# Weight units of 128x2048 in half as many buffers, in a fp32 two-block transformer on one core

## The chip, the core and the metric

The kernel runs on one core of a Trainium2 chip. Its engines are TensorE (PE: matmuls and transposes into PSUM), VectorE (DVE), ScalarE (ACT), GpSimd (POOL) and SyncE (SP), which here issues the loads of the weights. The metric is the device time of one execution in microseconds. The trace and its views come from one profiled execution.

## The reference, cut to what matters

256 tokens of 1024 features go through two blocks, all in fp32. The matrices are the weights that the change is about.

```python
# first block
h = rmsnorm(x, norm_mix)
(q, kc, vc, ks, vs, kw, vw, nsa_g, rq, rk, rv, rg, gate_a, gate_b) = split(h @ w_in)
nsa_out = nsa_mixer(rotary(q), rotary(kc), vc, ...)   # compress(): silu(blocks(k) @ ck_w1) @ ck_w2
ret_out = silu(rg) * retention(rq, rk, rv)
mix = sigmoid(gate_a) * (nsa_out @ w_proj_a) + sigmoid(gate_b) * (ret_out @ w_proj_b)
x = x + mix @ w_out
h = rmsnorm(x, norm_mlp)
x = x + square(relu(h @ w_up)) @ w_down               # hidden width 4096
x = rmsnorm(x, norm_final)
# second block
n = rmsnorm_2(h)
z, xBC, dt, q, k, v, r, a1, g_ssd, g_gla = split(n @ w_in)
merged = sigmoid(g_ssd) * (ssd_mixer(...) @ w_up_ssd) + sigmoid(g_gla) * (gla_mixer(...) @ w_up_gla)
h = h + merged @ w_o
h = h + mem_cross_attention(rmsnorm_2(h), rmsnorm_2(mem), w_xq, w_xkv, w_xo)
h = h + (silu(g) * u) @ w_ffn_out                     # g, u = split(rmsnorm_2(h) @ w_ffn_in), width 2816
return rmsnorm_2(h, norm_final)
```

## The kernel before

**Precision.** TensorE is to multiply fp32 values, but in its fp32r format. So each operand is split in a high part (a cast to fp32r) and a low part (the value less its high part), and each product is three matmuls: high by high, high by low, low by high. `load` does this for one unit of weights: SyncE loads it into a buffer `raw`, ScalarE casts `wh`, VectorE subtracts `wl` (L95 to L97 of before, L99 to L101 of after). A unit is 128 rows by up to UNIT columns: some 128-row blocks of a weight matrix, beside each other. Activations are split alike (`split`, L113) into pairs such as `hh`/`hl`, `gd`/`k2`.

**Buffers.** Each kind of tile has a ring of buffers (BUFS); a tile waits until an older one of its ring is free. `raw` has 4, `wh` and `wl` have 8 each, of 128x1024. So a unit's load waits for the subtraction of an older unit, and its cast for the matmuls of an older unit.

**Order.** The program writes the operations in an order of its own, and a framework then schedules each engine's queue, before the run, with the rings as one of its constraints. On each engine the instructions run in the order of that queue, which the sections below show in a few places.

**The GEMMs.** `gemm_tok` makes a token-major product of two column ranges for both halves of the tokens (it holds all its weights until the second half is done); `gemm_feat` and `s_feat` make feature-major products of 256 columns; `s_tok` is a token-major product of 512 columns that yields after each pair of 128-row blocks. The `stream` is a list of such products (`stream1`: rq, rk, rv, rg and the gates) from which other code draws pieces (`pump`, `need`), as work for TensorE while NSA or retention runs on other engines.

**NSA's prologue.** After the first norm, kv and q are projected (`gemm_tok`, 512 columns) and the gates and windows (280 columns). Keys are rotated (L356 to L359), doubled (L434), transposed and split. `compress` builds blocks of keys (L374, L381, L113) and multiplies them by `ck_w1` and later `cv_w1`, each in four loads of four 128-row blocks by 256 columns. rq and rk come from the stream at the same time; their rows are rotated on VectorE by the same lines L356 to L359 (128x512).

**w_down and w_ffn_out** (`Down`): the hidden rows come in parts of two 128-row blocks by 1024 columns. All but the last parts are added into four accumulators (two halves t of the tokens, two halves f of the columns) as they come. The last parts are held back (`late`), and then `finish` runs them half by half: all of (0, 0) and (0, 1), then the residual add (L845) and the norm of the first 128 tokens (squares L218, L220, L211 on GpSimd, products L230), while TensorE does (1, 0) and (1, 1). After w_down two norms follow each other, and then the transposes for the next projection.

Of the kernel before, what the change touches and what calls it, by code (L numbers as in the profile page):

```python
# [12 lines left out]
F32 = mybir.dt.float32  # L13
# [7 lines left out]
P = 128  # L21
EPS = 1e-6
NEG = -1e30
NUNITS = 314
UNIT = 1024
WARM = 14


# [6 lines left out]
G_MIX, G_MLP, G_FIN, G_MIX2, G_XATT, G_MEM, G_FFN, G_FIN2, G_SSD, G_GLA, G_NUM = range(11)  # L35

BUFS = dict(
    raw=4, wh=8, wl=8, hh=5, hl=5, xr=2, g2=9, k2=14, gd=10, sc=24,
)


# [10 lines left out]
class Builder:  # L52
# [36 lines left out]
    def load(self, w, c0, ncol, k, nk):  # L89
        nc = self.nc  # L90
        i = len(self.keys)
        self.keys.append((w, c0, ncol, k, nk))
        raw, wh, wl = self.T("raw", [P, UNIT]), self.T("wh", [P, UNIT], F32R), self.T("wl", [P, UNIT], F32R)
        m = nk * ncol
        nc.sync.dma_start(raw[:, :m], self.d["wbig"][i, :, :m])  # L95
        nc.scalar.copy(wh[:, :m], raw[:, :m])  # L96
        nc.vector.tensor_sub(wl[:, :m], raw[:, :m], wh[:, :m].bitcast(F32))  # L97
        cs = [slice(j * ncol, (j + 1) * ncol) for j in range(nk)]
        return [(wh[:, c], wl[:, c]) for c in cs]  # L99

    def units(self, w, c0, ncol, K, k0=0):  # L101
        n = UNIT // ncol
        return [x for k in range(k0, k0 + K, n) for x in self.load(w, c0, ncol, k, min(n, k0 + K - k))]

    def mm(self, out, lhsT, rhs, start, stop):
        self.nc.tensor.matmul(out, lhsT, rhs, start=start, stop=stop)  # L106
# [13 lines left out]
            self.mm(o, hi, wl, False, False)  # L120
            self.mm(o, lo, wh, False, k == K - 1)

    def gemm_tok(self, w, c0s, ncol, src, K=8, rest=None, mid=None, ahead=3, others=()):

        us, n = [], UNIT // ncol
        for c0 in c0s:
            us.append([])
            for k in range(0, K, n):  # L130

                with ExitStack() as order:
                    if rest and (c0 != c0s[0] or k >= ahead * n):
                        for x in self.first:
                            order.enter_context(self.tc.issue_after(x.ins))
                    us[-1] += self.load(w, c0, ncol, k, min(n, K - k))
                if c0 == c0s[0] and k // n in others:
                    others[k // n]()
        acc = [[self.PS("acc") for _ in range(2)] for _ in c0s]
        for t in range(2):  # L140
            if rest and t:
                rest()
            for g in range(len(c0s)):
                if mid and t and g == len(c0s) - 1:
                    mid(acc)
                self.tok_mm(acc[g][t][:, :ncol], src, us[g], t)
        return acc

    def s_tok(self, key, w, c0, ncol, src, done, K=8):

        acc = [self.PS("acc") for _ in range(2)]
        n = UNIT // ncol
        for k0 in range(0, K, n):
            ws = self.load(w, c0, ncol, k0, min(n, K - k0))
            for t in range(2):
                o = acc[t][:, :ncol]
                for j, (wh, wl) in enumerate(ws):
                    k = k0 + j
                    hi, lo = src.parts(k, slice(t * P, (t + 1) * P))
                    self.mm(o, hi, wh, k == 0, False)  # L160
                    self.mm(o, hi, wl, False, False)
                    self.mm(o, lo, wh, False, k == K - 1)
            if k0 + n < K:
                yield
        self.have[key] = done(acc)
        yield
# [329 lines left out]
    def nsa(self, hT, rest):  # L496
        nc, d = self.nc, self.d
# [5 lines left out]
        def small():  # L503
            for x, y in ((self.cst[:, P:], d["cst"][:, P:]), (self.cb, d["cb"]), (self.cm, d["cm"]), (self.posi, d["pos"]), (pa[:, :A_N], d["para"])):
                nc.sync.dma_start(x, y)
        akv, aq = self.gemm_tok("w_in", (0, 512), 512, hT, rest=rest, ahead=1, others={1: second, 3: small})
        self.rope_tables()
        kcT, vcT = [self.T("gd", [P, 2, 256]) for _ in range(2)]

# [64 lines left out]
        for t in range(2):  # L574
# [3 lines left out]
            sc = self.T("cbt", [P, 8, 15], bufs=2)  # L578
# [3 lines left out]
            m = self.S(8)  # L582
# [193 lines left out]
    class Down:  # L776
# [40 lines left out]
        def mm(self, i, hi, lo):  # L817
            if self.acc is None:
                self.acc = [[self.b.PS("acc") for _ in range(2)] for _ in range(2)]
            ws = self.b.units(self.w, 0, 1024, 2, 2 * i)  # L820

            def part(t, f):
                ts, fs, o = slice(t * P, (t + 1) * P), slice(f * 512, (f + 1) * 512), self.acc[t][f]
                for k, (wh, wl) in enumerate(ws):
                    kk = 2 * i + k
                    self.b.mm(o, hi[:, k, ts], wh[:, fs], kk == 0, False)
                    self.b.mm(o, hi[:, k, ts], wl[:, fs], False, False)
                    self.b.mm(o, lo[:, k, ts], wh[:, fs], False, kk == 2 * self.n - 1)
            if i < self.n - 4:
                for t in range(2):  # L830
                    for f in range(2):
                        part(t, f)
            else:
                self.late.append(part)
# [587 lines left out]
def wbig(W, keys):  # L1422
    out = np.zeros((NUNITS, P, UNIT), np.float32)
    for i, (w, c0, nc_, k0, nk) in enumerate(keys):
        out[i, :, :nk * nc_] = W[w][k0 * P:(k0 + nk) * P, c0:c0 + nc_].reshape(nk, P, nc_).transpose(1, 0, 2).reshape(P, nk * nc_)
    return out


def program(tc, d):
    with ExitStack() as ctx:  # L1430
        b = Builder(ctx, tc, d)
        b.start()
        b.block2(*b.block1())
    assert len(b.keys) == NUNITS, len(b.keys)
    return b.keys
# [14 lines left out]
```

## Time and profile before

| | before |
|---|---|
| median of 2 runs | 1003.13 us (1002.63 to 1003.64) |
| profiled execution | 1002.8 us, span 1001.0 us |
| mean granted clock of TensorE | 0.992 |
| TensorE, VectorE, ScalarE busy | 980.6, 661.9, 510.7 us |
| weight units | 314 |

The busy time is the sum over an engine's instructions within the span; the ends of matmuls are modelled, so that two matmuls in a row overlap in the rows. The granted clock is the share of full speed that TensorE was given. A row's "idle before" is the time that the engine stood still ahead of it, with the instruction that ended this.

### The profile page before, as it was taken

The numbers are of one execution on the slowest core, as the hardware profiler recorded it, in microseconds if no ns is written. First come the engines' busy times: TensorE is split into PE (matmuls) and PEld (weight loads), VectorE is DVE, ScalarE is ACT, GpSimd is POOL, SyncE is SP. The second block draws the span as 40 slices with busy tenths as digits, with TensorE's granted clock in tenths as the row PEclk, the third lists the DMA queues.
The fourth block names the chain that finished last, engine by engine and source line by source line (L and its number), as shares of the span: only waits on it lengthen the run. The fifth ranks groups of instructions, "written<-read, shape, count | busy, mean of one in ns | idle before, by whom it ended". The sixth has DMA issues, their size and how long they took to land.

```text
span 1001.0 us, 16172 instructions
## 1 busy us (share of the span) xinstructions
PE 980.6 (98%) x6388; PEld 876.9 (88%) x6388; DVE 661.9 (66%) x994; ACT 510.7 (51%) x797; POOL 53.8 (5%) x80
## 2 busy tenths in 40 slices
PE   8999999899999999999999989999999999999997
PEld 5878999787888899789898888998998879899995
DVE  6798768866755555678878666677756467455543
ACT  5656546635644444465765535555545345444432
POOL 1000100000000000100010231200000000000000
PEclk8999999999999999999999999999999999999999
DMA  7656744233655666276446442753755157556531
GB/s 274 213 195 223 253 138 146 87 128 126 221 190 185 200 215 195 106 251 199 155 147 190 148 148 85 253 191 128 229 190 187 45 190 248 193 169 203 177 126 42
DMA packets 49212, 174.92 MB, mean 175 GB/s; under 512 B 5984, under 2 KB 6240, under 8 KB 49136
## 3 DMA queue, kind: packets, MB, share of 16 engines
q1 hardware_dynamic: 46512, 166.15, 50.5%
q0 software_dynamic: 2192, 6.94, 2.2%
q8 instruction: 50, 0.82, 0.3%
q10 hardware_dynamic: 432, 0.79, 0.2%
q14 instruction: 26, 0.21, 0.1%
HBM read 172.81 MB, written 1.05 MB: 174 GB/s over the span
## 4 chain that ended last, share of the span: by engine, by line
PE 90%; DVE 5%; ACT 2%; DMA 2%; issue 1%; POOL 0%; POOLq 0%; ACTq 0%; DVEq 0%
PE acc L106 64%; PE sm L106 23%; PE sm L110 2%; DVE wl L97 2%; PE po L106 1%; DMA raw<-in_wbig_dram 1%; ACT wh L96 1%; DMA k<-in_gains_dram 1%; ACT hh L113 0%; DVE hl L113 0%; ACT k L629 0%; DVE k L113 0%; DVE gd L555 0%; DVE sc L625 0%; PE po L110 0%
## 5 line engine op out<-in xcount | busy, mean ns | idle before, releaser
L97 DVE TENSOR_TENSOR wl<-raw,wh 128x1024 fp32r<-128x1024 f32 (+1 forms) x314 | 379.5, 1221 | 214.7 <-ACT wh L96 213.4
L96 ACT CAST wh<-raw 128x1024 fp32r<-128x1024 f32 (+1 forms) x314 | 325.5, 1049 | 292.7 <-PE acc L106 133.7
L106 PE MATMUL acc<-hh,wh 128*128 128x256 f32 x736 | 207.2, 283 | 3.8 <-ACT g L271 3.3
L106 PE MATMUL acc<-hh,wl 128*128 128x256 f32 x736 | 207.5, 282 | 0.0
L106 PE MATMUL acc<-hl,wh 128*128 128x256 f32 x736 | 206.4, 281 | 0.0
L106 PE MATMUL acc<-wl,hh 128*128 128x512 f32 (+1 forms) x400 | 158.1, 396 | 0.7 <-DVE wl L97 0.7
L106 PE MATMUL acc<-wh,hh 128*128 128x512 f32 (+1 forms) x400 | 156.7, 397 | 1.2 <-ACT hh L113 1.1
L106 PE MATMUL acc<-wh,hl 128*128 128x512 f32 (+1 forms) x400 | 156.4, 396 | 0.0
L106 PEld LDWEIGHTS acc<-hh,wh 128*128 128x128 f32 x736 | 138.4, 189 | 5.4 <-ACT g L271 3.5
L106 PEld LDWEIGHTS acc<-hl,wh 128*128 128x128 f32 x736 | 139.1, 189 | 0.2
L106 PEld LDWEIGHTS acc<-hh,wl 128*128 128x128 f32 x736 | 139.0, 189 | 0.3 <-issue 0.2
L106 PE MATMUL sm<-hh,wl 128*128 128x256 f32 x488 | 136.5, 280 | 0.0
L106 PE MATMUL sm<-hl,wh 128*128 128x256 f32 x488 | 136.4, 279 | 0.0
L106 PE MATMUL sm<-hh,wh 128*128 128x256 f32 x488 | 136.4, 279 | 0.0
L106 PEld LDWEIGHTS sm<-hl,wh 128*128 128x128 f32 x488 | 91.7, 188 | 0.8
L106 PEld LDWEIGHTS sm<-hh,wh 128*128 128x128 f32 x488 | 91.4, 187 | 0.9
L106 PEld LDWEIGHTS acc<-wh,hh 128*128 128x128 f32 x400 | 75.7, 190 | 18.6 <-ACT hh L113 2.7
L106 PEld LDWEIGHTS acc<-wl,hh 128*128 128x128 f32 x400 | 76.0, 190 | 18.2 <-DVE wl L97 1.9
L106 PEld LDWEIGHTS sm<-hh,wl 128*128 128x128 f32 x488 | 91.6, 188 | 0.0
L106 PEld LDWEIGHTS acc<-wh,hl 128*128 128x128 f32 x400 | 75.9, 190 | 17.9 <-DVE hl L113 1.1
L106 PE MATMUL acc<-wl,gd 128*128 128x512 f32 x216 | 85.4, 396 | 0.0
L106 PE MATMUL acc<-wh,gd 128*128 128x512 f32 x216 | 85.1, 395 | 0.0
(292 smaller groups left out, 1079.4 us busy)
## 6 DMA issues: line engine op xcount, KB each, us to landing
raw<-in_wbig_dram SPq DMA_DIRECT2D x311, 512.0 KB, 4.1
k<-in_gains_dram POOLq DMA_DIRECT2D x18, 256.0 KB, 4.5
k<-in_mem_dram POOLq DMA_DIRECT2D x4, 256.0 KB, 5.6
raw<-in_wbig_dram SPq DMA_DIRECT2D x2, 420.0 KB, 3.8
k<-in_decay_dram POOLq DMA_DIRECT2D x4, 192.0 KB, 5.1
xr<-in_x_dram SPq DMA_DIRECT2D x1, 512.0 KB, 6.6
out_dram<-k SPq DMA_DIRECT2D x2, 256.0 KB, 2.5
out_dram<-k ACTq DMA_DIRECT2D x2, 256.0 KB, 2.7
```

Source lines behind the costliest of these rows:

```text
L96: nc.scalar.copy(wh[:, :m], raw[:, :m])
L97: nc.vector.tensor_sub(wl[:, :m], raw[:, :m], wh[:, :m].bitcast(F32))
L106: self.nc.tensor.matmul(out, lhsT, rhs, start=start, stop=stop)
L110: self.nc.tensor.transpose(out, src, self.ident[:n, :n])
```

## The change

UNIT goes from 1024 to 2048, and `raw`, `wh` and `wl` have half as many buffers (2, 4, 4): the same memory. 166 units are left of 314. The first unit is loaded, cast and subtracted in two halves. `gemm_tok` lets two units go ahead of the first norm instead of three, and the hooks that load the second half of x and the small tensors stand behind the units 0 and 1 (before: 1 and 3). `s_tok` still yields after each pair of blocks, but loads only every fourth block. `Down` holds back the last two parts instead of four. 147 of the 166 units are wider than 1024 columns; the compress weights (eight loads), the two projections with 512 inputs, and a small one stay at 1024 or less, each in a buffer of 2048.

```diff
-NUNITS = 314
-UNIT = 1024
+NUNITS = 166
+UNIT = 2048
...
-    raw=4, wh=8, wl=8, hh=5, hl=5, xr=2, g2=9, k2=14, gd=10, sc=24,
+    raw=2, wh=4, wl=4, hh=5, hl=5, xr=2, g2=9, k2=14, gd=10, sc=24,
...
-        nc.sync.dma_start(raw[:, :m], self.d["wbig"][i, :, :m])
-        nc.scalar.copy(wh[:, :m], raw[:, :m])
-        nc.vector.tensor_sub(wl[:, :m], raw[:, :m], wh[:, :m].bitcast(F32))
+        n = 2 if i == 0 else 1
+        for h in range(n):
+            c = slice(h * m // n, (h + 1) * m // n)
+            nc.sync.dma_start(raw[:, c], self.d["wbig"][i, :, c])
+            nc.scalar.copy(wh[:, c], raw[:, c])
+            nc.vector.tensor_sub(wl[:, c], raw[:, c], wh[:, c].bitcast(F32))
...
-    def gemm_tok(self, w, c0s, ncol, src, K=8, rest=None, mid=None, ahead=3, others=()):
+    def gemm_tok(self, w, c0s, ncol, src, K=8, rest=None, mid=None, ahead=2, others=(), unit=UNIT):
...
-        us, n = [], UNIT // ncol
+        us, n = [], unit // ncol
...
-        for k0 in range(0, K, n):
-            ws = self.load(w, c0, ncol, k0, min(n, K - k0))
+        for k0 in range(0, K, 2):
+            if k0 % n == 0:
+                ws = self.load(w, c0, ncol, k0, min(n, K - k0))
             for t in range(2):
                 o = acc[t][:, :ncol]
-                for j, (wh, wl) in enumerate(ws):
-                    k = k0 + j
+                for k in (k0, k0 + 1):
+                    wh, wl = ws[k % n]
...
-        akv, aq = self.gemm_tok("w_in", (0, 512), 512, hT, rest=rest, ahead=1, others={1: second, 3: small})
+        akv, aq = self.gemm_tok("w_in", (0, 512), 512, hT, rest=rest, ahead=1, others={0: second, 1: small})
...
-            if i < self.n - 4:
+            if i < self.n - 2:
```

The schedule moves with it. VectorE in the NSA prologue, before, around the first subtraction for rk (`wl_748`; `gd_339` and `gd_340` are scaled queries, `gd_336` values):

```order
L113 TENSOR_TENSOR gd_336<-acc_380,gd_335 128x2x64
L358 TENSOR_TENSOR rtmp_579<-k_131_574,ropes_328 128x2x8
L555 TENSOR_TENSOR gd_339<-sm_460,gd_339 64x2x128
L97 TENSOR_TENSOR wl_748<-raw_746,wh_747 128x1024
L97 TENSOR_TENSOR wl_766<-raw_764,wh_765 128x1024
L359 TENSOR_TENSOR k_131_574<-rtmp_578,rtmp_579 128x2x16
L555 TENSOR_TENSOR gd_340<-sm_460,gd_340 64x2x128
```

The same engine and place after, where the first subtraction for rk is `wl_709` (`k_123_577` is the block of keys for compress, `acc_455` and `acc_456` are the two halves of rq that are being rotated):

```order
L386 TENSOR_SCALAR k_127_597<-cst_90 128x4x34 x2
L361 TENSOR_TENSOR k_141_664<-acc_455,ropec_306 128x512
L362 TENSOR_TENSOR k_142_665<-acc_455,ropes_307 128x4x64
L363 TENSOR_TENSOR k_142_665<-acc_455,ropes_307 128x4x64
L101 TENSOR_TENSOR wl_693<-raw_691,wh_692 128x1024
L117 TENSOR_TENSOR k_124_582<-k_123_577,k_124_582 128x4x30
L117 TENSOR_TENSOR k_125_587<-k_123_577,k_125_587 128x4x30
L117 TENSOR_TENSOR k_126_592<-k_123_577,k_126_592 128x4x30
L117 TENSOR_TENSOR k_127_597<-k_123_577,k_127_597 128x4x30
L560 TENSOR_TENSOR gd_318<-sm_505,gd_318 64x2x128
L364 TENSOR_TENSOR k_140_663<-k_141_664,k_142_665 128x512
L361 TENSOR_TENSOR k_145_678<-acc_456,ropec_306 128x512
```

Two more rope rows (L362, L363) stand between the last of these and `wl_709`. The first rk subtraction has moved from ahead of the preparation of compress to behind it and behind the rope of both halves of rq; 12 subtractions with 17600 columns stand ahead of it, where before 24 with 23744 columns stood ahead of the last of those rope rows.

TensorE where the compress matmuls begin, before (`acc_745` is rk, `sm_635` the compress accumulator):

```order
L106 MATMUL acc_745<-wh_884,hh_102 128x512
L106 MATMUL acc_745<-wl_885,hh_102 128x512
L106 MATMUL acc_745<-wh_884,hl_104 128x512
L106 MATMUL sm_635<-wh_637,k_142_615 128x256
L106 MATMUL sm_635<-wl_638,k_142_615 128x256
```

And after (`acc_705` and `acc_706` are rk, `sm_602` is the compress accumulator):

```order
L110 MATMUL acc_706<-wl_709,hh_101 128x512
L110 MATMUL acc_706<-wh_708,hl_103 128x512
L110 MATMUL acc_706<-wh_708,hh_101 128x512
L114 MATMUL sm_570<-cst_90,k_122_571 128x128 x2
L110 MATMUL sm_602<-wh_604,k_124_582 128x256
```

Before, all 48 matmuls of rk's eight blocks stand between rq and compress; after, 22 of its first unit do.

TensorE at the end of w_down, before, at the last matmul of the first 128 tokens (`acc_3064`) and the first of the other 128 (`acc_3065`):

```order
L106 MATMUL acc_3064<-wh_4241,gd_4206 128x512
L106 MATMUL acc_3064<-wl_4242,gd_4206 128x512
L106 MATMUL acc_3064<-wh_4241,k_846_4207 128x512
L106 MATMUL acc_3065<-wh_4112,gd_3942 128x512
L106 MATMUL acc_3065<-wl_4113,gd_3942 128x512
```

And after (`acc_2881` is the first 128 tokens, `acc_2882` and `acc_2883` the others):

```order
L110 MATMUL acc_2881<-wh_3950,gd_3927 128x512
L110 MATMUL acc_2881<-wl_3951,gd_3927 128x512
L110 MATMUL acc_2881<-wh_3950,k_681_3928 128x512
L110 MATMUL acc_2882<-wh_3950,gd_3927 128x512
L110 MATMUL acc_2882<-wl_3951,gd_3927 128x512
```

From the first row of the other 128 tokens to the transposes of the norm, 48 matmuls stood before and 15 stand after.

## Rows read from the trace of the kernel before

**Rows 1.** The page: busy time (share of the span) by engine, chain that ended last.

```profile
PE 980.6 (98%) x6388; PEld 876.9 (88%) x6388; DVE 661.9 (66%) x994; ACT 510.7 (51%) x797; POOL 53.8 (5%) x80
PE 90%; DVE 5%; ACT 2%; DMA 2%; issue 1%; POOL 0%; POOLq 0%; ACTq 0%; DVEq 0%
```

**Rows 2.** Instructions by line and shape: busy us, mean ns of one, idle before.

```profile
L97 DVE TENSOR_TENSOR wl<-raw,wh 128x1024 fp32r<-128x1024 f32 x311 | 376.8, 1224 | 214.6 <-ACT wh L96 213.4
L113 DVE TENSOR_TENSOR k<-k,gd 128x512 fp32r<-128x512 f32 x12 | 8.3, 693 | 8.2 <-ACT gd L113 8.2
L96 ACT CAST wh<-raw 128x1024 fp32r<-128x1024 f32 x311 | 323.2, 1051 | 292.7 <-PE acc L106 133.7 <-issue 85.2 <-PE sm L106 45.9
L113 ACT CAST gd<-k 128x512 fp32r<-128x512 f32 x12 | 7.4, 620 | 16.2 <-DVE k L765 16.2
```

**Rows 3.** DMA issues of raw: KB each, median us from issue to landing.

```profile
raw<-in_wbig_dram SPq DMA_DIRECT2D x311, 512.0 KB, 4.1
raw<-in_wbig_dram SPq DMA_DIRECT2D x1, 280.0 KB, 3.6
```

**Rows 4.** Waits of SyncE's DMA queue: us in total, times, longest.

```profile
SPq L95 <- DVE wl L97: 736.4, 270, 21.7
```

**Rows 5.** Busy us of each engine by windows, then granted clock, DMA share, GB/s.

```profile
core 0: us, PE busy (x) PEld busy (x) DVE busy (x) ACT busy (x) POOL busy (x), PEclk, DMA share, GB/s
40.00:60.00 20.00, 20.00 (x113) 17.23 (x112) 18.61 (x44) 15.31 (x27) 0.00 (x0) 1.00 0.83 283
66.00:70.40 4.40, 2.10 (x10) 1.20 (x8) 4.34 (x10) 2.13 (x4) 0.00 (x0) 0.99 0.58 196
70.40:73.70 3.30, 3.25 (x8) 2.60 (x9) 2.93 (x5) 0.00 (x0) 0.00 (x0) 0.50 0.60 175
183.00:204.00 21.00, 17.85 (x130) 14.97 (x129) 15.86 (x45) 10.99 (x35) 1.14 (x2) 1.00 0.16 51
260.00:395.00 135.00, 135.00 (x866) 121.72 (x865) 74.97 (x79) 63.70 (x78) 2.19 (x4) 1.00 0.61 201
```

**Rows 6.** Timeline of TensorE: rq's first matmul, and 69 to 71 us.

```profile
45.16 0.48 PE L106 MATMUL acc<-wh,hh 128*128 128x512 f32 x1
...
69.32 0.44 PE L110 MATMUL sm<-cst,k 128*128 128x128 f32 x2 [1.65 <-DVE hl L113]
70.45 0.80 PE L106 MATMUL acc<-wl,hh 128*128 128x512 f32 x1 [0.69 <-DVE wl L97]
```

**Rows 7.** Timeline of VectorE, 62 to 69 us.

```profile
63.02 1.22 DVE L97 TENSOR_TENSOR wl<-raw,wh 128x1024 fp32r<-128x1024 f32 x1
...
64.92 1.22 DVE L97 TENSOR_TENSOR wl<-raw,wh 128x1024 fp32r<-128x1024 f32 x1
...
67.59 0.41 DVE L358 TENSOR_TENSOR k<-acc,ropes 128x256 f32<-128x256 f32 x1
```

**Rows 8.** Timelines of VectorE and TensorE at the end of w_down.

```profile
407.08 0.69 DVE L845 TENSOR_TENSOR xr<-acc,xr 128x512 f32<-128x512 f32 x1 [0.47 <-PE acc L106]
409.46 1.41 DVE L230 SCALAR_TENSOR_TENSOR xr<-xr,sc,k 128x512 f32<-128x512 f32 x2 [0.68 <-POOL sc L211]
413.29 1.41 DVE L230 SCALAR_TENSOR_TENSOR g<-xr,sc,k 128x512 f32<-128x512 f32 x2
...
417.62 0.40 PE L106 MATMUL acc<-wl,gd 128*128 128x512 f32 x1
417.85 0.39 PE L106 MATMUL acc<-wh,k 128*128 128x512 f32 x1
418.08 1.03 PE L110 MATMUL sm<-cst,g 128*128 128x128 f32 x8
419.36 0.50 PE L106 MATMUL acc<-wh,hh 128*128 128x512 f32 x1 [0.24 <-ACT hh L113]
```

More of the change, by code (lines that the diff above doesn't have):

```diff
@@ L162, in s_tok @@
                     self.mm(o, lo, wh, False, k == K - 1)
-            if k0 + n < K:
+            if k0 + 2 < K:
                 yield
```

## The prediction

> **What bounds the kernel now.** I read the busy times and the chain that ended last first [rows 1]: TensorE is busy 980.6 us of a span of 1001.0, and 90% of the chain lies on it. VectorE and ScalarE are busy 66% and 51%, and of the chain they hold 5% and 2%. So the kernel is bound by its matmuls, and a change that touches no matmul can gain only from the 20 us in which TensorE is idle, and can lose by making it wait more. The second view, instructions by line and shape, says what a unit of weights costs [rows 2]: a cast of 1051 ns on ScalarE and a subtraction of 1224 ns on VectorE per 128x1024, 311 times. The DMA issues give the load [rows 3], and the waits say who holds the ring: the queue that loads raw waits for the subtraction of the unit that had the buffer before, 270 times, 736.4 us in all [rows 4]. That wait costs nothing by itself: in 260 to 395 us TensorE is busy 135.00 of 135.00 us [rows 5]. Next come the places where it is not. In 66 to 70.4 us it is busy 2.10 of 4.40 us, behind VectorE (4.34 of 4.40), and in 70.4 to 73.7 us the granted clock is 0.50, the lower of its two levels, 1.2 GHz [rows 5]. The timeline has the gaps: 1.65 us before a transpose of NSA keys and 0.69 before the first matmul of the next weight, both behind VectorE [rows 6]. Another 3.15 us are idle in 183 to 204 us [rows 5].
>
> **What gets lighter.** Twice the columns in one instruction save a fixed part. The nearest rows are the 512-column split of the same kind [rows 2]: the cast goes from 620 to 1051 ns and the subtraction from 693 to 1224 ns for 512 columns more. So I estimate a 2048-column cast at 1051 + 2 x 431 = 1913 ns and a subtraction at 1224 + 2 x 531 = 2286 ns, against 2102 and 2448 for two of 1024. Of 166 units 147 are wider than 1024, so some 28 us leave ScalarE and 24 us VectorE. Nearly all of it lies beside matmuls. Where VectorE is what TensorE waits for (40 to 75 us, and 183 to 204 us) it counts; the first is in the walk below. For the second and all others I take -2, between 0 and -5 (the idle time there, 3.15, and some of the gaps at the changes of GEMM).
>
> **The ring in steady stretches.** A 2048-column unit feeds 24 matmuls of 512 columns, which start 0.23 us apart [rows 8], 5.6 us. Two raw buffers allow 11.2 us for load, cast and subtraction of one unit. A load of 1 MB I estimate at 5.2 us: from 280 to 512 KB it grew from 3.6 to 4.1 [rows 3], so 512 KB more are worth 1.1. 5.2 + 1.9 + 2.3 = 9.4, so 1.8 us are left, where four buffers of 1024 had 11.2 - 6.4 = 4.8. The MLP and the FFN (about 135 us of each like 260 to 395) should stay full: 0 for them, and the rest of this goes to a rival. The Trainium skill, DMA: Bandwidth & Descriptors (Bandwidth), gives 6.15 us for a 1 MB load on another kind of queue and asks for transfers of at least 1 MiB; with its price the ring would take 10.4 us, still under 11.2, and the sum would be the same with a higher chance for that rival.
>
> **The start.** The first unit comes in halves, so the first matmuls wait for the same 1024 columns as before. The later ones have two raw buffers instead of four, and each is split for 1.93 us longer (1913 + 2286 - 1051 - 1224 ns) before a matmul can read it. I take +1.0, between 0 and 1.9.
>
> **The NSA prologue, 46 to 110 us, is where the change costs.** The wh and wl rings have four buffers, and the compress weights (256 columns, four rows of blocks, one load each) fill only half of one: eight of those loads stand among 2048-column ones. Before, eight buffers held them beside the next projections. The order shows the result: before, 48 rk matmuls stand between the last rq matmul and the first compress matmul, and the first rk subtraction stands on VectorE ahead of the whole preparation of compress (L374, L381). After, 22 rk matmuls stand there, and the first rk subtraction stands behind that preparation and behind both sets of rope multiplies. TensorE reaches its first rk matmul after rq: rq starts at 45.16 us now [rows 6] and 1 us later then; 48 matmuls of 0.233 us are 11.2, and 20 transposes 2.4 more (eight take 1.03 [rows 8]), so at about 59.8 us. When is the subtraction ready? The rows before have the same instructions: the last rope multiply (L358) ends at 68.0 us [rows 7]. VectorE had subtracted 23744 columns in 24 instructions ahead of it; after it has 17600 in 12. At 1.037 ns for a column and 162 ns for an instruction this is 8.3 us less work. In 40 to 60 us VectorE is busy 18.61 of 20.00 us [rows 5], so work that is gone comes off nearly whole, 59.7; with the late start 60.7, and if it waits for every load that now goes out later (each behind the subtraction that frees one of two buffers), 64.3 by a walk through the queue. The subtraction takes 2.3 more: TensorE waits until 63.0 at best and 66.6 at worst, 3.2 to 6.8 us, and I take 6.
>
> The same pattern comes back while compress and rk, rv, rg share the four buffers: the two small matmuls on the compressed keys, the second rk unit, a transpose of rope rows, the rv units. Walking the queues with the durations of [rows 2, 3] I get 2.0, 2.2, 1.0, 2.7 and 1.6 us, 9.5 in all; at the other end half of them is hidden by the lighter VectorE, 3 us. I take 8. Against this stand the gaps of the same work before, 3.0 us. So the prologue is +11 (6 + 8 - 3), between +3.2 and +13.3. The rule that speaks against the change is in the Trainium skill, Perfetto Trace Analysis (Optimizing Scalar/DVE Operations): where these engines are not saturated but cause gaps on others, breaking up instructions may let work complete sooner. By that rule alone, with five waits each longer by the 1.93 us of one wider split, the term would be +9.7, and the sum 1 us lower.
>
> **The last rows of w_down.** Two parts of 2 blocks by 1024 columns are held back instead of four: 48 late matmuls instead of 96. After the last matmul of the first rows 48 stand before the transposes now, 15 in the new order: 11.2 and 3.5 us of cover. The chain that they cover goes from the residual add at 407.08 to the end of the second scaled product, 413.29 + 1.41 = 414.70 [rows 8], less the foreign add of 0.69: 6.9 us. Before, the transposes start at 418.08, when the last matmul is done, with no gap. Now 6.9 - 3.5 = 3.4 us are open, and the clock may fall as it did after the gap at 67 us, where 3.3 us at half speed cost 1.65. I take +4, between 2.5 and 5.1. In the FFN's last rows the same cover ends the kernel, where nothing follows: 0.
>
> **Other changes of GEMM** (w_out to w_up, w_o to the queries, w_xo to the FFN): a GEMM of two column halves holds all four wide buffers, so the next weight is cast only when one is free, and its split takes 1.93 us longer. Gaps there are now like the 0.24 us ahead of 419.36 [rows 8]. I take +0.5 each, 1.5, between 0 and 4. The new loads per 2 blocks inside the token stream move no matmul: 0.
>
> **The sum.** 1002.8 (the profiled execution, span 1001.0 and 1.8 around it) + 1.0 + 11 + 4 + 1.5 - 2 = 1018.3; the median of the two runs shown is 0.3 higher than that execution. The walk counts each wait to the full, so I round down: **1018 us**.
>
> **Rivals.** *The prologue hides it* (1002 to 1009): VectorE is lighter by 8.3 us just there, and if the loads go out early enough the subtraction ends at 63.0 and the later waits are short: +1 + 3.2 + 2.5 - 2 = 1007.5 or less. For it speaks VectorE's load in 40 to 60 us; against it the order, in which TensorE has nothing to do ahead of that subtraction. *Faster than before* (about 999): the chain from the NSA keys to compress runs through VectorE, and less work on it takes off both the 3 us of gaps at 67 to 70 us and the 1.65 at half clock, and 2.5 at 183 to 204 us, with +1 for the start and +2.5 for w_down: 1002.8 - 3 - 1.65 - 2.5 + 3.5 = 999. It decides at one point: the first rk subtraction must be done by 59.8 us, 3.2 earlier than my best bound. *The ring starves* (1028 and more): 1.8 us are left per unit; where ScalarE or VectorE does more than that ahead of a split in the MLP, the FFN or the projections, each unit is late. 1 us on 20 of the 148 and the prologue's upper end give 1028. Against it, both engines have idle time in each such stretch, VectorE 60 of 135 us [rows 5]. *The wide instruction saves nothing*: 2048 columns cost as much as twice 1024, then the gain of 2 and the 1.9 us of saved instructions in the prologue go, 1021.
>
> **How the numbers follow.** The forecast (1010 to 1027) has 0.50, the hidden prologue 0.22, faster than before 0.12, the starved ring 0.12, no saving 0.04. From 1000 to 1029 leaves out most of the starved ring and half of the gain, 0.15 to 0.2. The bound for a change that a measurement tells is 2%, 983 and 1023. Slower: a quarter of the forecast, the starved ring and a little, 0.27. Faster: 0.02. Within: 0.71.
>
> **What would show it.** Of the profile after I expect a first idle time of 3 to 7 us before an rk matmul, ended by the subtraction, at 59.8 to 67 us; about 16 us of gaps in 46 to 110 us, with the clock at half once or twice; a gap of 3 to 4 us before the transposes after w_down; the cast near 1913 and the subtraction near 2286 ns; the load near 5.2 us; a stretch like 260 to 395 us that is full. The prediction is wrong if the prologue's gaps stay near 3 us, or if gaps that end on a subtraction stand all through the MLP and the FFN.

## The result, and the profile after

The changed kernel takes 1046.16 us, median of 2 runs (1043.03 to 1049.29): slower, with a ratio to before of 1.0443, 95% interval 1.0398 to 1.0488. The profiled execution is the slower of the two, with a span of 1047.5 us, 46.5 more than before.

From the page of the changed kernel, busy times by engine and the chain that ended last, as [rows 1] of before:

```profile
PE 1000.4 (96%) x6388; PEld 890.6 (85%) x6388; DVE 648.8 (62%) x847; ACT 488.2 (47%) x650; POOL 50.9 (5%) x80
PE 82%; DVE 7%; DMA 4%; ACT 4%; issue 2%; POOL 0%; SPq 0%; POOLq 0%; ACTq 0%; DVEq 0%
```

The two engines that split did get lighter (VectorE by 13.1 us, ScalarE by 22.5; the estimates were 24 and 28), and the kernel slower. The same 6388 matmuls are busy for 19.8 us longer, since more of them run at the lower clock (mean granted clock 0.974, before 0.992) or stand alone behind a gap; the other 26.7 us of the longer span are idle time. TensorE's share of the chain fell from 90% to 82%; VectorE, ScalarE and the loads have 2% more each.

What one unit costs, by line and shape (busy us, mean ns, idle before) and in the DMA issues (KB, us to landing), as [rows 2, 3]:

```profile
L101 DVE TENSOR_TENSOR wl<-raw,wh 128x2048 fp32r<-128x2048 f32 x146 | 334.3, 2291 | 210.9 <-ACT wh L100 208.6 <-PE sm L114 1.9
L100 ACT CAST wh<-raw 128x2048 fp32r<-128x2048 f32 x146 | 278.5, 1909 | 266.9 <-PE acc L110 111.1 <-PE sm L110 75.3 <-DMA raw<-in_wbig_dram 74.4
raw<-in_wbig_dram SPq DMA_DIRECT2D x146, 1024.0 KB, 4.8
```

The estimates were 2286 and 1913 ns and 5.2 us. The Trainium skill, VectorE: DVE Perf Modes (The TRN2 errata — SBUF-src ops pay a fixed extra latency per instruction), gives (columns + 151) / 0.96 ns for an fp32 add of two tensors; that is 2291 ns for 2048, and the subtraction in this trace agrees. The last field of the cast is the news: the wide casts alone wait 74.4 us for loads of raw; over casts of all widths it is 80.7 us, and before it was 24.4.

Windows of the changed kernel (busy us of each engine, granted clock, DMA share, GB/s), as [rows 5]:

```profile
60.00:80.00 20.00, 13.28 (x73) 11.00 (x70) 13.97 (x32) 7.53 (x16) 0.00 (x0) 0.83 0.24 81
80.00:100.00 20.00, 15.86 (x70) 12.24 (x70) 13.20 (x22) 7.87 (x11) 0.00 (x0) 0.83 0.47 165
100.00:120.00 20.00, 18.31 (x79) 14.35 (x78) 9.55 (x8) 9.41 (x10) 0.00 (x0) 0.91 0.60 221
200.00:220.00 20.00, 15.11 (x104) 11.85 (x102) 14.94 (x49) 10.74 (x40) 1.14 (x2) 1.00 0.33 109
220.00:240.00 20.00, 15.62 (x108) 14.79 (x108) 13.12 (x17) 8.18 (x9) 0.00 (x0) 0.87 0.27 89
300.00:440.00 140.00, 140.00 (x866) 124.94 (x865) 74.62 (x54) 63.39 (x54) 2.19 (x4) 1.00 0.57 200
440.00:460.00 20.00, 16.49 (x68) 12.80 (x67) 14.46 (x18) 10.07 (x20) 1.66 (x3) 0.91 0.19 69
620.00:640.00 20.00, 15.88 (x109) 15.01 (x109) 13.82 (x16) 6.74 (x10) 9.28 (x11) 0.85 0.48 178
880.00:1020.00 140.00, 140.00 (x981) 130.37 (x980) 75.01 (x54) 59.02 (x46) 0.00 (x0) 1.00 0.55 192
```

Two things are to be seen. The long stretches of the MLP and the FFN are as full as before (140.00 of 140.00 us at full clock, twice). The loss is in a few places, and there it is double: idle time, and a clock below 1.00 in the same window or the next. In the 60 us of the first three windows TensorE is idle for 12.55 us, and the granted clock is 0.83, 0.83 and 0.91.

To place the loss I added up the matmuls of both traces in their order, each at its duration at full clock, and compared the times at which both had done the same amount. The lag of the changed kernel in us, gained in each stage (the stages end where before is at 50, 135, 199, 261, 401, 422, 565 and 673 us):

```text
kernel         start  prologue  NSA tail  w_out  MLP  w_down  SSD   GLA   rest   sum
forecast       +1.0   +11       -2        +0.5   0    +4      0     0     +1.0   +15.5
changed        +1.1   +16.7     +3.7      +8.5   +0.3 +4.9    +4.1  +6.4  -0.2   +45.5
```

The -2 of the forecast stands for all gains together; it is under the NSA tail, where most of them were expected. The last columns are stretches of time (before, SSD is 422 to 565 us and GLA 565 to 673), and the end of the SSD mixer itself falls in the column GLA.

The first gap is where it was forecast. The timelines of TensorE and VectorE at the first rk matmuls, as [rows 6, 7]:

```profile
63.13 0.73 PE L110 MATMUL acc<-wh,hh 128*128 128x512 f32 x2 [2.92 <-ACT wh L100]
67.20 0.80 PE L110 MATMUL acc<-wl,hh 128*128 128x512 f32 x1 [3.34 <-DVE wl L101]
```

```profile
64.54 0.41 DVE L363 TENSOR_TENSOR k<-acc,ropes 128x256 f32<-128x256 f32 x1
64.87 2.28 DVE L101 TENSOR_TENSOR wl<-raw,wh 128x2048 fp32r<-128x2048 f32 x1
```

The subtraction stands behind the last rope multiply and ends at 67.15; TensorE waits 6.26 us in two pieces, first for the cast, then for the subtraction.

The w_out product, which was forecast at half a microsecond, has a gap of 3.60 us. Timelines of ScalarE, VectorE and TensorE there, and two windows:

```profile
228.47 1.91 ACT L100 CAST wh<-raw 128x2048 fp32r<-128x2048 f32 x1 [2.72 <-PE acc L110]
...
230.81 1.89 ACT L100 CAST wh<-raw 128x2048 fp32r<-128x2048 f32 x1
237.61 1.90 ACT L100 CAST wh<-raw 128x2048 fp32r<-128x2048 f32 x1 [4.90 <-DMA raw<-in_wbig_dram]
239.41 1.67 ACT L874 ACTIVATE hh<-g 128x512 fp32r<-128x512 f32 x3
241.59 1.90 ACT L100 CAST wh<-raw 128x2048 fp32r<-128x2048 f32 x1 [0.51 <-DMA raw<-in_wbig_dram]
```

```profile
230.41 2.29 DVE L101 TENSOR_TENSOR wl<-raw,wh 128x2048 fp32r<-128x2048 f32 x1 [0.41 <-ACT wh L100]
...
234.42 2.28 DVE L101 TENSOR_TENSOR wl<-raw,wh 128x2048 fp32r<-128x2048 f32 x1
236.62 0.69 DVE L870 TENSOR_TENSOR g<-g,g 128x512 f32<-128x512 f32 x1
```

```profile
235.56 0.40 PE L110 MATMUL acc<-wh,hl 128*128 128x512 f32 x1
239.56 1.22 PE L110 MATMUL acc<-wh,hh 128*128 128x512 f32 x2 [3.60 <-ACT wh L100]
```

```profile
235.50:240.00 4.50, 0.90 (x3) 0.46 (x3) 4.07 (x6) 2.39 (x3) 0.00 (x0) 0.78 0.80 288
240.00:243.00 3.00, 3.00 (x8) 2.35 (x8) 3.00 (x4) 2.49 (x4) 0.00 (x0) 0.50 0.41 137
```

Two units are cast one after the other; the third has no raw buffer until the first is subtracted, at 232.70. Its load lands 4.8 us later and its cast, which waits 4.90 us for that, is done at 239.51. TensorE has not used up the two units that it has by then: ahead of the gap it runs 6 of the 24 matmuls of the first one, those on the first of four pieces of mix. The other pieces come late. The sum for the second (L870) stands on VectorE behind the second unit's subtraction, and the copies of the last three in fp32r (L874) stand on ScalarE behind the third unit's cast. So TensorE stands still until the third unit is there, and the matmuls behind the gap run at half clock (0.50, 1.2 GHz).

After w_down, as [rows 8], TensorE waits for the norm, and in SSD for a small activation; the third row is the longest gap of the column GLA. Timelines of TensorE and of ScalarE:

```profile
452.16 1.09 PE L114 MATMUL sm<-cst,g 128*128 128x128 f32 x6 [3.48 <-DVE g L235]
...
520.33 0.38 PE L110 MATMUL acc<-hh,wh 128*128 128x256 f32 x1 [1.78 <-ACT gd L1131]
...
634.68 0.58 PE L110 MATMUL acc<-hh,wh 128*128 128x256 f32 x1 [4.12 <-ACT g L276]
```

```profile
517.63 0.48 ACT L1131 ACTIVATE gd<-acc,par 128x256 f32<-128x256 f32 x1
518.00 1.90 ACT L100 CAST wh<-raw 128x2048 fp32r<-128x2048 f32 x1
519.79 0.49 ACT L1131 ACTIVATE gd<-acc,par 128x256 f32<-128x256 f32 x1
```

The second activation of L1131, which TensorE waits for, stands behind a cast of 1.90 us on ScalarE. The gap in GLA was there before too, with 3.29 us instead of 4.12.

### The profile page after: what moved, and what is told of

It is laid out like the page before. It is cut to its first block, busy times and chain, and to the rows that moved or that the text cites. A ratio compares the mean times of both kernels' runs of the same rounds, so it can differ in the third digit from the quotient of the medians.

```text
span 1047.5 us, 15306 instructions
## 1 busy us (share of the span) xinstructions
PE 1000.4 (96%) x6388; PEld 890.6 (85%) x6388; DVE 648.8 (62%) x847; ACT 488.2 (47%) x650; POOL 50.9 (5%) x80
## 4 chain that ended last, share of the span: by engine, by line
PE 82%; DVE 7%; DMA 4%; ACT 4%; issue 2%; POOL 0%; SPq 0%; POOLq 0%; ACTq 0%; DVEq 0%
PE acc L110 60%; PE sm L110 20%; DMA raw<-in_wbig_dram 4%; DVE wl L101 3%; ACT wh L100 3%; PE sm L114 2%; PE po L110 1%; ACT k L634 1%; DVE k L117 0%; DVE sc L630 0%; DVE k L640 0%; DVE k L361 0%; DVE k L1182 0%; DVE hl L117 0%; POOL sc L216 0%
## 5 line engine op out<-in xcount | busy, mean ns | idle before, releaser
L101 DVE TENSOR_TENSOR wl<-raw,wh 128x2048 fp32r<-128x2048 f32 (+2 forms) x167 | 359.9, 2157 | 229.4 <-ACT wh L100 227.1
L100 ACT CAST wh<-raw 128x2048 fp32r<-128x2048 f32 (+2 forms) x167 | 300.4, 1802 | 293.3 <-PE acc L110 129.8
L110 PE MATMUL acc<-hh,wh 128*128 128x256 f32 x736 | 209.8, 286 | 6.4 <-ACT g L276 4.1
L110 PE MATMUL acc<-hl,wh 128*128 128x256 f32 x736 | 208.8, 284 | 0.0
L110 PE MATMUL acc<-wh,hh 128*128 128x512 f32 (+1 forms) x400 | 161.2, 408 | 8.6 <-ACT wh L100 7.5
L110 PE MATMUL acc<-wl,hh 128*128 128x512 f32 (+1 forms) x400 | 161.6, 406 | 7.5 <-DVE wl L101 7.5
L110 PE MATMUL acc<-wh,hl 128*128 128x512 f32 (+1 forms) x400 | 158.7, 401 | 0.8 <-DVE hl L117 0.8
L110 PEld LDWEIGHTS acc<-wl,hh 128*128 128x128 f32 x400 | 78.3, 196 | 26.7 <-DVE wl L101 10.1
```

What stands on the lines that cost most here:

```text
L100: nc.scalar.copy(wh[:, c], raw[:, c])
L101: nc.vector.tensor_sub(wl[:, c], raw[:, c], wh[:, c].bitcast(F32))
```

## The experiments

The theory after the first look (**grain**): in the stages where TensorE takes units in bursts, a wider unit comes later, since its cast and its subtraction are one long instruction each, and since a buffer of 2048 columns is free only when all of it has been used. Rivals: the missing cover after w_down, the half-filled buffers of compress, the load itself. Each time is a median; "before" ran beside them at 1001.1 to 1001.4 us. With each edit the queues are scheduled anew, so a run compares two kernels with their orders, and not one instruction alone.

**Cover after w_down.** The changed kernel with four parts held back, and the kernel before with two:

```diff
-            if i < self.n - 2:
+            if i < self.n - 4:
```

> The changed kernel, with the last four parts of w_down and w_ffn_out held back again (each part is now one wide unit, so all four wh and wl buffers are held). If the missing cover costs the lag of about 5 us that the changed kernel takes on at the end of w_down (a gap of 3.63 us and slow matmuls behind it), the gap goes and the time falls to about 1041. Rival: the next weights find no free buffer while four are held, so a gap of 2 to 4 us comes back behind the transposes, and the time stays at 1044 to 1047.

> The kernel before, with the last two parts of w_down and w_ffn_out held back instead of four, and nothing else. If the cover alone makes the gap, TensorE waits 3.4 to 3.6 us ahead of the transposes after w_down and runs 1.6 us slower behind: 1007 to 1009. Rival: with 1024-column units the next weights come early and fill the gap, 1003.

Measured: 1042.12 us (ratio to before 1.0402, interval 1.0356 to 1.0448), and 1003.80 (1.0027, 1.0014 to 1.0041). In the kernel before the shorter cover makes a gap that is there, but small:

```profile
418.84 1.29 PE L110 MATMUL sm<-cst,g 128*128 128x128 f32 x8 [1.53 <-DVE g L230]
```

1.53 us instead of the 3.4 to 3.6 expected, a lag of 1.8 us at that place, and the time is near the rival's 1003. In the changed kernel the gap ahead of the transposes goes with four parts, but one of 1.92 us comes back behind them, as its rival said, and the lag there is 3.3 instead of 4.9. So cover is worth about 2 us; the forecast put 4 on it. The 4 us that a_late4 is faster lie mostly elsewhere in its profile (w_out and GLA in the table below), so that its time is near the 1041 expected is luck. b_late2 also serves as a bound for everything but the buffers: apart from the first loads (the look-ahead of `gemm_tok`, the hooks, the first unit in halves) it is the changed program with 1024-column units, and it is 2.7 us slower than before.

**Width of the instructions, or of the load.** Three kernels with the same four wide wh and wl and two wide raw buffers. Halves for all three (`a_half`), for cast and subtraction only (`a_onedma`), for the load only (`a_dmahalf`):

```diff
-        n = 2 if i == 0 else 1
+        n = 2 if m == 2048 else 1
```

> The changed kernel, with every unit of 2048 columns loaded, cast and subtracted in two halves of 1024 in the same wide buffers. If the width of the instructions is what makes TensorE wait (a split of 4.2 us before the first matmul instead of 2.3), about half of the 17 us of the prologue and of the 8 us around w_out come back: 1030 to 1035. If it is the number of buffers (a buffer is free only when all of it has been used, and only two loads are under way), little comes back, 1043 to 1048, with some 24 us more VectorE time than the changed kernel.

> The changed kernel, each wide unit loaded in one DMA of 1 MB, but cast and subtracted in two halves. Halving all three took 21 us off the changed kernel. If the width of the cast and the subtraction is what makes TensorE wait, most of it comes off here too: 1024 to 1030. If it is the load (the first half of a unit lands earlier when it is asked for alone), 1038 to 1046.

> The other half of that: each wide unit loaded in two DMAs of 512 KB, but cast and subtracted in one instruction each. If the width of the instructions is the cause, 1042 to 1048, as the changed kernel; if the load is, 1024 to 1032.

Measured: a_half 1025.06 us (ratio 1.0231, 1.0192 to 1.0271), a_onedma 1025.32 (1.0239, 1.0218 to 1.0261), a_dmahalf 1051.84 (1.0504, 1.0476 to 1.0532). The width of the two instructions, with the order that comes with it, is worth 21 us, nearly half of the loss, and more than a_half's expectation gave it (1030 to 1035). Halving the load gives nothing back: a_half is level with a_onedma, and a_dmahalf is 5.7 us slower than the changed kernel, above its range. In a_half the wait for the first rk subtraction is 1.73 instead of 3.34 us and the wait for the cast before it 0.64 instead of 2.92:

```profile
59.04 0.73 PE L110 MATMUL acc<-wh,hh 128*128 128x512 f32 x2 [0.64 <-ACT wh L100]
61.50 0.79 PE L110 MATMUL acc<-wl,hh 128*128 128x512 f32 x1 [1.73 <-DVE wl L101]
```

The prologue's lag falls from 16.7 to 9.4 us, w_out's from 8.5 to 1.9, the NSA tail's from 3.7 to -1.3. VectorE and ScalarE are busy 659.2 and 504.7 us, nearly as before the change: the saving is given back, and it was worth nothing.

**Which ring.** raw in four buffers of 1024 beside wide wh and wl (`a_rawnarrow`), and two wide raw buffers with loads of 1 MB beside eight wh and wl of 1024 (`a_rawwide`):

```diff
 # a_rawnarrow, raw=4
+            raw = self.T("raw", [P, 1024])[:, :m // n]
 # a_rawwide, wh=8, wl=8
+            wh, wl = self.T("wh", [P, 1024], F32R), self.T("wl", [P, 1024], F32R)
```

> The changed kernel with four raw buffers of 1024 columns: each wide unit is loaded, cast and subtracted in two halves, each half through a raw buffer of its own, while wh and wl stay four buffers of 2048. If the wide raw buffers (two loads under way, each freed only when both halves are subtracted) make what is left after halving, the time falls to 1006 to 1012. If it is the four wide wh and wl buffers, it stays at 1020 to 1027.

> The opposite: two raw buffers of 2048 with one load of 1 MB for each (the first unit in halves), and eight wh and wl buffers of 1024, cast and subtracted 1024 columns at a time. If the wide raw buffers are the cause, 1015 to 1027; if the wide wh and wl buffers are, 1003 to 1010.

Measured: 1025.63 us (1.0242, 1.0211 to 1.0274) and 1019.21 (1.0178, 1.0129 to 1.0228). Each time lies in the range that lays the rest on the ring that is still wide, so neither ring alone makes it. The stages tell more than the sums (table below): what a_half had left in the prologue (9.4) and at w_out (1.9) is 2.4 and 0.2 with narrow raw, but also 4.5 and 0.0 with narrow wh and wl, so either ring made narrow takes most of it away. In SSD and GLA narrow raw is as bad or worse, +5.6 and +10.6 for 6.2 and 3.3.

**Half-filled buffers.** The compress weights in two loads of eight blocks, in the changed kernel (`a_pack`) and in a_half (`a_half_pack`):

```diff
-            for j, (wh, wl) in enumerate(self.load(w1, 0, 256, 4 * q, 4)):
+            if q % 2 == 0:
+                ws = self.load(w1, 0, 256, 4 * q, 8)
+            for j, (wh, wl) in enumerate(ws[4 * (q % 2):4 * (q % 2) + 4]):
```

> The changed kernel with the compress weights in two loads of eight blocks (2048 columns) instead of four loads of four, so that no half-filled buffer stands in the prologue; nothing else changes. If half-filled buffers make the prologue's lag of 17 us, half or more of it goes: 1034 to 1038. Rival: the buffers are held as long and the first compress matmul waits for a wider split: 1043 to 1048.

> The kernel with all units split in halves, and the compress weights in two loads of eight blocks. If the half-filled buffers are what is left of the prologue (9 us), 1017 to 1021; if not, 1024 to 1027.

Measured: 1033.98 us (1.0326, 1.029 to 1.0361) and 1026.38 (1.025, 1.022 to 1.028). In the changed kernel the prologue falls from 16.7 to 6.3 us, and the time is at the lower end of its expectation: the half-filled buffers had a part in 10.4 us of it. Halving the instructions took 7.3 off the same 16.7, so the two causes overlap. In a_half the prologue falls too, from 9.4 to 3.6, but GLA takes 7.4 more, so that the time says nothing: the expectation was wrong on the sum and right on the prologue.

**How sharp the raw ring is in the kernel before.** Two, three and five raw buffers of 1024 (for five, two k2 buffers or one hh buffer are given up), and the shorter k2 ring alone:

```diff
-    raw=4, wh=8, wl=8, hh=5, hl=5, xr=2, g2=9, k2=14, gd=10, sc=24,
+    raw=5, wh=8, wl=8, hh=5, hl=5, xr=2, g2=9, k2=12, gd=10, sc=24,
```

> The kernel before, with two raw buffers of 1024 columns instead of four, wh and wl as they were. A buffer's cycle is 4.1 + 1.05 + 1.22 = 6.4 us, so two give a unit every 3.2 us and TensorE takes one every 2.8: if the load's latency and the number of raw buffers set the rate, even the steady stretches starve by 0.4 us per unit, and the time is 1080 to 1130. Rival: only the bursts lose (prologue, w_out), because the wh and wl rings cover the rest: 1010 to 1040.

> The kernel before with three raw buffers of 1024 columns. Two cost 62 us in this kernel. Three give a unit every 6.4 / 3 = 2.1 us, against 2.8 that TensorE takes: if only the steady rate counts, nothing is lost, 1001 to 1003; if bursts and the time that a buffer waits for VectorE and ScalarE count, 1008 to 1025.

> The kernel before with five raw buffers of 1024 columns instead of four; the memory for it is taken from the k2 ring (12 instead of 14 buffers). If the raw ring is what bursts wait for, the kernel before has a little of it left (in the start and in the prologue), and this gains 1 to 4 us: 997 to 1000. Rival: four are enough, and a shorter k2 ring costs as much or more: 1001 to 1008.

> The kernel before with 12 k2 buffers instead of 14, raw as before. With five raw buffers paid for by these two, the prologue gained 2.7 us and SSD and GLA lost 17. If the shorter k2 ring is the cause of that loss, it is here too: 1010 to 1018. If the order that comes with another raw ring is, the time is that of the kernel before: 1000 to 1004.

> Five raw buffers again, the memory now taken from the hh ring (4 instead of 5 buffers), k2 at 14. If k2 was the cause of the loss in SSD and GLA, this keeps the prologue's gain alone: 997 to 1000. If any new order of the queues loses there, since TensorE has little other work in that stage, 1005 to 1016.

Measured: two 1064.13 us (1.0621, 1.0584 to 1.0659), three 1011.87 (1.0105, 1.0084 to 1.0126), five 1014.97 (1.0121, 1.008 to 1.0163) and with hh 1009.72 (1.0087, 1.0058 to 1.0116), the k2 ring alone 1003.31 (1.0019, 1.0006 to 1.0032). With two buffers even the MLP is not full:

```profile
280.00:300.00 20.00, 19.05 (x117) 16.76 (x117) 12.73 (x19) 11.58 (x19) 0.00 (x0) 1.00 0.58 200
340.00:420.00 80.00, 75.88 (x475) 68.53 (x474) 39.89 (x40) 35.17 (x41) 2.18 (x4) 0.96 0.56 185
```

4.1 us in 80 are far from the 0.4 per 2.8 that the cycle of 6.4 us in two buffers would give, so most of the time the wh and wl rings cover it; the time is below the expected 1080 to 1130 and above its rival's 1010 to 1040. Three buffers came out as expected from bursts (1008 to 1025). Five buffers have -2.7 and -4.8 us in the start and the prologue together, but the k2 ring alone has -2.3 in its one profile and no gain in its times, so that a gain is not clear; and they lose 15 and 9 us in SSD and GLA, where the k2 ring alone loses 0.5. Both times lie above the 997 to 1000 of a gain, the first also above its rival's 1008, the second within its rival's 1005 to 1016. So this loss comes with another raw ring, with more buffers as with fewer. More buffers should only let a unit come earlier in the same queues, which points to the new order of the queues; no run had the old order with the new ring, so that is argued and not shown. None of the 14 kernels is faster than the one before.

The lag by stages, worked out as above, in us:

```text
kernel         start  prologue  NSA tail  w_out  MLP  w_down  SSD   GLA   rest   sum
changed         1.1    16.7      3.7       8.5   0.3   4.9     4.1   6.4  -0.2   45.5
a_late4         0.4    16.6      3.7       5.8   0.3   3.3     4.3   1.7  -0.2   35.9
a_dmahalf       1.8    17.7      4.0       8.0   0.1   6.7     5.3   1.6   1.3   46.5
a_half         -0.4     9.4     -1.3       1.9   0.3   2.8     6.2   3.3  -0.1   22.1
a_onedma       -0.2     9.5     -1.0       4.2  -0.3   3.7     4.7   2.0  -0.8   21.8
a_pack          1.3     6.3      0.9       6.8   0.1   5.1     4.6   6.2  -0.2   31.1
a_half_pack    -0.8     3.6     -1.4       2.4   0.2   3.7     4.3  10.7  -0.2   22.5
a_rawnarrow    -0.7     2.4     -1.4       0.2   1.8   2.8     5.6  10.6  -0.1   21.2
a_rawwide      -0.3     4.5     -0.4       0.0  -0.3   1.8     2.2   6.7  -0.5   13.7
b_late2        -0.8    -0.2      0.0       0.1  -0.1   1.8     0.1  -0.2  -0.1    0.6
b_raw2          0.7    13.4      2.1       0.0   9.8   1.9    10.4   4.1  18.7   61.1
b_raw3         -0.4     3.0     -0.2       0.0   0.3   0.0     2.1   4.6  -0.5    8.9
b_raw5         -1.9    -0.8      2.8       0.0   0.0   0.0     3.8  10.8   0.0   14.7
b_raw5_hh4     -2.4    -2.4      2.9       0.0   0.0   0.0     4.7   4.6   0.0    7.4
b_k12          -1.0    -1.3     -0.1       0.0   0.0   0.0     0.0   0.5   0.0   -1.9
```

Each row is one profile, and differences of a few microseconds in it can be the clock of that execution. On TensorE, VectorE and ScalarE the changed kernel and a_late4 run the same operations in the same order up to w_down. In w_out they are idle 5.08 and 4.96 us, but the granted clock is 0.93 and 0.97, and the lags are 8.5 and 5.8. In GLA, where their orders differ, they are idle 6.04 and 6.20 us, at 0.96 and 0.98, and the lags are 6.4 and 1.7. So only differences well above 3 to 5 us, or those that a gap shows too, are read as effects here.

So the theory of the grain holds for about half of the loss by the width of the instructions (a_half, a_onedma), and with the half-filled buffers and the two wide rings it covers most of the lag of the prologue and of w_out. For SSD and GLA no run shows what makes it.

## Why the prediction was wrong, step by step

The direction was right, and so was the mechanism of the first gap, but the size was not: 1046 us lie outside of the range that ended at 1029. Of the 30 us between the forecast's +15.5 and the +45.5, SSD and GLA have 10.5, w_out 8.0, the prologue 5.7 and the NSA tail 5.7.

- **What bounds the kernel, and the steady stretches**: right. The MLP and the FFN lose 0.3 us and nothing. The rival of the starved ring (1028 and more) takes in the measured time, but by a mechanism that isn't there; b_raw2 shows what it would look like.
- **The lighter engines**: the price of a wide instruction was right (1909 and 2291 ns), its worth was not. VectorE's busy time fell by 13.1 us where 24 were estimated, and none of it was seen in the time. -2 was put on the places where TensorE waits for VectorE; the NSA tail lost 3.7 us instead, and a_half, with the old width, has -1.3 there. What counts in such a place is how early a result is there, and a wide instruction delivers later; the gaps at w_out and in SSD show this, in the tail it is argued from a_half alone.
- **The start**: +1.1 for +1.0. rq begins at 46.30 us, before at 45.16. That it is so near is in part luck: b_late2 and before, with the same order there, differ by 0.8 in this column.
- **The prologue** was mis-sized: 16.7 for 11 (3.2 to 13.3). The first gap was 6.26 for 6, with the subtraction at 64.87 where the walk had 64.3. Over the stage TensorE is idle 12.58 us (51.1 to 152.8 us) where it was 2.34 (50 to 135), 10.2 more, so the net gaps of 11 were nearly right. The other 6.5 us are the same matmuls being busy for longer, which the term left out: three windows at 0.83, 0.83 and 0.91 of the clock. The clock is priced only once, for w_down.
- **The last rows of w_down**: 4.9 for 4, with a gap of 3.48 for 3.4. The reason was only half right: b_late2 shows 1.8 us for the shorter cover alone, and the rest came with the wide units.
- **Other changes of GEMM** was the step that failed most for its size: 8.5 for 0.5 at w_out (5.8 in a_late4's profile, with the same order). It took a gap like the 0.24 us of before and a split that is 1.93 us later. It left out that the third unit's load cannot go out before the first subtraction, so that its cast is done 6.8 us after that (232.70 to 239.51), that the small instructions for mix stand behind wide ones on VectorE and ScalarE, and the half clock behind the gap. With halved instructions the 8.5 fell to 1.9, with narrow raw buffers or narrow wh and wl besides to 0.2 and 0.0. For w_o and w_xo the forecast of half a microsecond each was not far off.
- **SSD and GLA** were put at nothing without a reason: 10.5 us. One new gap was read (ScalarE, the small activation behind a wide cast). In GLA the idle time grew by only 1.8 us (from 4.28 to 6.04); the rest of the 6.4 is slower matmuls, which a_late4 doesn't have. Beyond that it stays open which step of the new order makes the loss: each kernel with another ring of raw, or of wh and wl, has between 6 and 16 us there, also with the old width, and the k2 ring alone 0.5.
- **The rule on breaking up instructions** of the Trainium skill, Perfetto Trace Analysis (Optimizing Scalar/DVE Operations), was weighed at +9.7 us, in the prologue alone. a_onedma agrees with it: broken up, the same loads in the same buffers give back 21 us. That is still less than half of the loss.

## What to carry to other kernels

Where an engine was off the critical path, what it saved in busy time was worth nothing here, and what it delivered later was paid where its consumer waited. So test a wider unit at the changes of stage and not by the steady rate: look there for the small instructions that stand behind a wide one in a queue, and for the loads that wait until a wide one is done. A buffer ring is to be counted in units and in bytes: half as many buffers of twice the size hold less when some units fill only half, and they come free in bigger steps. Price a gap in TensorE with the slower matmuls behind it: here the idle time grew by 26.7 us and the busy time of the same matmuls by 19.8. And before a stage's time is compared between two profiles, split it in idle and busy time: in the two stages compared above the idle time came back within 0.2 us, and the lag did not.

## What the runs showed of the hardware

A small VectorE multiply becomes up to five times longer while GpSimd works on tensors of its own. Timeline of the kernel before, VectorE and then GpSimd, at the end of SSD:

```profile
585.11 0.25 DVE L1177 TENSOR_SCALAR k<-gd,gdec 128x64 f32<-128x64 f32 x1
585.28 1.33 DVE L1178 TENSOR_SCALAR k<-gd,gdec 128x64 f32<-128x64 f32 x1
...
587.13 0.73 DVE L1177 TENSOR_SCALAR k<-gd,gdec 128x64 f32<-128x64 f32 x1
587.79 1.34 DVE L1178 TENSOR_SCALAR k<-gd,gdec 128x64 f32<-128x64 f32 x1
```

```profile
584.03 5.04 POOL L469 TENSOR_TENSOR g<-g,k 128x512 f32<-128x512 f32 x4 [2.40 <-DMA k<-in_gains_dram]
```

The four instructions of GpSimd's product end at 585.30, 586.55, 587.81 and 589.07, and the four multiplies end about 0.06 us behind them, whenever they began: one that begins with such an instruction takes 1.33 or 1.34 us, one that begins later in it 0.73 or 0.25. Where no such product runs, at 612.48 to 613.21 us, the same multiply takes 0.24 to 0.25 us four times. In the changed kernel, where the product runs from 624.34 to 630.98, three of four take 1.33 us, and the fourth, which begins as it ends, 0.24. In a_rawnarrow they begin as the product ends, and all four take 0.24. This is next to the longest gap of the column GLA in both kernels; that it makes the gap was not tried.
